# POOL's subtracts and scalings in pieces of 128 or 256 columns, merged V evacuation, and the second key head's rows moved beside the first steps

## The chip, the cores and the metric

The kernel runs on one core of a Trainium2 chip. Its time is the device time of one execution in microseconds (us); for a kernel with several runs it is their median. The engines are named as in the profile: PE (TensorE, matmuls and transposes), PEld (its weight loads), DVE (VectorE), ACT (ScalarE), POOL (GpSimd), SP (SyncE, which issues the DMAs).

## What is computed

A trunk of two layers over 512 latent tokens (a grid of 8 rows by 64 columns) and 256 context tokens, model width 1024. Each layer normalizes and modulates both streams, projects them with one wide matrix, and runs three branches whose gated outputs are merged, projected and added back:

```python
hx = rms_norm(x, norm_w) * (1.0 + scale_x) + shift_x
rq, rk, rv, rg, nq, nk, nv, ng, gq, gk, gv, gg, mg = split_cols(hx @ w_in)
# retention: 4 heads, both directions, chunks of 128, state from the context
# neighbourhood attention: 8 heads of 64, window 8 x 16 with a bias table, plus all context keys
p = softmax(concatenate([q @ k_local * scale + bias, q @ k_ctx * scale]))
# grouped attention: 8 query heads on 2 key heads, rms norm and rotary on q and k
o = softmax(q_g @ k_all.T * scale) @ v_all
m = g_ret * (ret_o @ w_ret_o) + g_na * (na_o @ w_na_o) + g_gqa * (gqa_o @ w_gqa_o)
x = x + gate_x * (m @ w_out)
```

The context stream gets the same treatment in the first layer only; a last rms norm ends the trunk. All is float32.

## The kernel before

**Split operands.** Every matmul operand is split into two parts of the fast 32-bit matmul type, a high part (the rounded value) and a low part (value minus high part). A product of two such operands is three matmuls, high by high, high by low and low by high (L289 to L291); with an attention probability as one operand it is two. ACT makes most high parts, by a copy, and DVE or POOL the low parts, by a subtract.

**Weights.** `_load` (L262 to L277) fetches a 128x1024 block by DMA into `raw` (two buffers) and makes two halves of 512 columns: `whi` by an ACT copy (L273) and `wlo` by a subtract on POOL (L275). In the finishing stages (`lo_dve` set) the second half's subtract goes to DVE. Each part has five buffers, and a load runs one to two blocks ahead of the matmuls. A block's k-th 128 columns are the k-th product's operand (`wk`, L296). In the last stage `load_b` (L1533 to L1540) splits four blocks of the output matrix in the same way.

**Order of work.** PE's order is written by hand: `window()` lays the steps of one attention head (scores, transposes, value products) between projection units, by costs in us. The orders of ACT, DVE and POOL come from a tile scheduler by priority; the weights' splits carry a raised one (`PRI`). The profiled execution goes through: input, statistics and first projections (0 to 60 us), neighbourhood attention of layer 0 (60 to 275), grouped attention (275 to 360), retention, merging and the finish of layer 0 with the layer change around 970, neighbourhood attention of layer 1 (995 to 1170), grouped attention (1170 to 1345), the rest (to 1640) and the finish.

**Neighbourhood attention.** `s_step` (L666 to L691) computes the scores of one of four query blocks of 128 against 512 keys, adds the bias while it takes the row maximum, and after each pair of blocks does negation (L684), exponentials on ACT (L686), reciprocal (L688) and the scaling of the two probability tiles (L691): even block on DVE, odd block on POOL, 512 columns as two groups of 256. `t_step` (L698) transposes them on PE into PSUM, and `split_pt` (L511) makes the high part on ACT (L514) and the low part on DVE (L515), for the value products L714 and L715. L615 and L616 copy rows of K's parts to the other half of the partitions. The context's own scaling (L537, POOL, 256 columns) and its transposes (L545) belong to the steps of layer 0.

**Grouped attention.** `k_fin` (L847 to L854) ends the key path: rotary, then for each of two key heads i the high part (L851, ACT), the low part (L852, DVE) and copies of both to the other 64 partitions (L853, L854, DVE), 64x768 each. `u_v` (L856 to L875) projects V, copies the projection to SBUF (L863), transposes it in blocks of 128 tokens (L868; groups of four and two blocks share a PSUM bank) and evacuates each block by one ACT copy (L872) and one DVE subtract (L873). In `steps` the scores of a query head (L935, L936) leave through DVE (L937, row maximum), two exponentials on ACT (L946), reciprocal (L948) and the scaling of two tiles of 768 columns (L951): the first on DVE, the second on POOL. `t_step` takes 256 keys at a time (L959), `pv_step` multiplies by V (L971). Query heads 0 to 3 (pairs p = 0, 1) read key head 0, the others key head 1. ACT's evacuations behind V's are L1174 in layer 0 and L1206 in layer 1.

## Time and profile before

| | |
|---|---|
| median of 3 runs | 1699.99 us (1697.99 to 1700.96) |
| the profiled execution's own time | 1703.24 us |
| its span, first to last instruction | 1701.5 us |
| mean granted clock of PE | 0.994 |
| busy: PE, DVE, ACT, POOL | 97%, 65%, 47%, 33% |
| read from memory, written | 138.41 MB, 4.19 MB |

PE is the fullest engine. The span is cut into the stages named above; what PE's busy time leaves of a stage is its idle time there. A bracket behind a timeline row tells the idle time ahead of an instruction and what released it.

### The profile page before, as it was taken

The page shows a single profiled execution, that of the slowest core. Times are in us where ns is not written, and L with a number is a line of the kernel's source. Part 1 is how long each engine was busy: PE and PEld are TensorE (multiplying, and loading weights), DVE is VectorE, ACT ScalarE, POOL GpSimd, SP SyncE. Part 2 cuts the span into 40 slices and gives each one's busy share as a digit, 9 for nine tenths or more (in the row PEclk, how much of TensorE's full clock was granted, in tenths as well). Part 3 has the DMA queues.
Part 4 walks back from the last instruction along what each step waited for, and adds up shares of the span by engine and source line. Part 5 has one row for each costly group of instructions (what it writes and reads, how often), then busy time and mean ns, then how long its engine had stood idle before and what let it go on. Part 6 is the DMA issues. An engine that isn't in the chain of part 4 may idle for free. (4 is left out here: it accounts for less than half of the span.)

```text
span 1701.5 us, 24925 instructions
## 1 busy us (share of the span) xinstructions
PE 1642.6 (97%) x9304; PEld 1409.8 (83%) x9304; DVE 1103.7 (65%) x2359; ACT 792.5 (47%) x1561; POOL 556.1 (33%) x482
## 2 busy tenths in 40 slices
PE   6999999999999999999999999999999999999997
PEld 4878888989998888888888889877888888888876
DVE  6666565757654566666768956666776645666775
ACT  4455563645553344443223545653555534444442
POOL 1433322333233222222232433432333333333542
PEclk9999999999999999999999999999999999999999
DMA  8211111111112111112635521211111121221641
GB/s 324 85 50 57 59 38 63 39 38 48 40 38 73 51 50 50 56 57 91 245 118 202 175 90 48 99 50 63 50 50 50 52 85 63 74 74 63 218 154 62
DMA packets 41881, 144.21 MB, mean 85 GB/s; under 512 B 4896, under 2 KB 6048, under 8 KB 40096
## 3 DMA queue, kind: packets, MB, share of 16 engines
q1 hardware_dynamic: 41760, 142.62, 23.6%
q8 instruction: 73, 1.20, 0.3%
q14 instruction: 48, 0.39, 0.1%
HBM read 138.41 MB, written 4.19 MB: 84 GB/s over the span
## 5 line engine op out<-in xcount | busy, mean ns | idle before, releaser
L275 POOL TENSOR_TENSOR wlo<-raw,whi 128x512 fp32r<-128x512 f32 x333 | 445.2, 1341 | 907.8 <-ACT whi L273 861.2
L289 PE MATMUL pj<-hxh,whi 128*128 128x512 f32 (+1 forms) x1232 | 444.9, 361 | 2.0 <-ACT mt L1206 1.9
L291 PE MATMUL pj<-hxh,wlo 128*128 128x512 f32 (+1 forms) x1232 | 429.4, 349 | 0.0
L290 PE MATMUL pj<-hxl,whi 128*128 128x512 f32 (+1 forms) x1232 | 428.2, 348 | 0.0
L273 ACT CAST whi<-raw 128x512 fp32r<-128x512 f32 x352 | 216.2, 619 | 291.2 <-PE pj L290 163.9
L291 PEld LDWEIGHTS pj<-hxh,wlo 128*128 128x128 f32 x1232 | 233.0, 189 | 31.9
L289 PEld LDWEIGHTS pj<-hxh,whi 128*128 128x128 f32 x1232 | 233.4, 189 | 21.2 <-ACT mt L1206 2.3
L290 PEld LDWEIGHTS pj<-hxl,whi 128*128 128x128 f32 x1232 | 233.9, 190 | 19.4
L515 DVE TENSOR_TENSOR pl<-pt,ph 128x512 fp32r<-128x512 f32 (+2 forms) x208 | 126.9, 625 | 54.4 <-ACT ph L514 52.7
L514 ACT CAST ph<-pt 128x512 fp32r<-128x512 f32 (+2 forms) x208 | 107.5, 533 | 65.7 <-PE pt L703 30.1
L289 PE MATMUL pj<-gat,whi 128*128 128x512 f32 (+1 forms) x260 | 91.5, 352 | 1.5 <-ACT mt L1174 1.5
L291 PE MATMUL pj<-gat,wlo 128*128 128x512 f32 (+1 forms) x260 | 89.8, 345 | 0.0
L290 PE MATMUL pj<-gat,whi 128*128 128x512 f32 (+1 forms) x260 | 89.5, 344 | 0.0
L937 DVE TENSOR_SCALAR_CACHE_REDUCE p<-s 128x384 f32<-128x384 f32 x128 | 68.9, 554 | 30.7 <-PE s L936 29.5
L946 ACT ACTIVATE p<-p,nm,rq 128x768 f32<-128x768 f32 x64 | 65.5, 1024 | 47.2 <-DVE nm L944 46.6
L290 PE MATMUL pt<-hxl,whi 128*128 128x512 f32 (+1 forms) x216 | 81.5, 377 | 2.5 <-DVE hxl L480 2.5
L289 PE MATMUL pt<-hxh,whi 128*128 128x512 f32 (+1 forms) x216 | 81.4, 377 | 1.0 <-ACT hxh L479 1.0
L291 PE MATMUL pt<-hxh,wlo 128*128 128x512 f32 (+1 forms) x216 | 80.9, 375 | 0.0
L951 POOL TENSOR_SCALAR p<-p,rc 128x768 f32<-128x768 f32 x32 | 40.3, 1260 | 76.8 <-DVE rc L948 48.4
L515 DVE TENSOR_TENSOR pl<-pf,ph 128x512 fp32r<-128x512 f32 (+1 forms) x56 | 45.4, 811 | 29.8 <-ACT ph L514 29.7
L514 ACT CAST ph<-pf 128x512 fp32r<-128x512 f32 (+1 forms) x56 | 32.9, 588 | 63.2 <-DVE pf L1111 63.2
L959 PE MATMUL pt<-ident,p 128*128 128x128 f32 x384 | 58.5, 273 | 2.0 <-POOL p L951 1.2
(425 smaller groups left out, 3547.4 us busy)
## 6 DMA issues: line engine op xcount, KB each, us to landing
raw<-in_wcol_dram SPq DMA_DIRECT2D x116, 512.0 KB, 3.5
araw<-in_adaw_dram SPq DMA_DIRECT2D x12, 1024.0 KB, 9.7
raw<-in_wbr_dram SPq DMA_DIRECT2D x24, 512.0 KB, 3.5
avw<-in_adav_dram SPq DMA_DIRECT2D x24, 512.0 KB, 3.7
raw<-in_wout_dram SPq DMA_DIRECT2D x24, 512.0 KB, 3.5
raw<-in_wv_dram SPq DMA_DIRECT2D x16, 512.0 KB, 3.5
bias<-in_nabias_dram SPq DMA_DIRECT2D x16, 384.0 KB, 3.0
x<-in_xt_dram SPq DMA_DIRECT2D x8, 384.0 KB, 5.9
```

Source lines behind the costliest of these rows:

```text
L273: nc.scalar.copy(hi, raw[:, c])
L275: lo_eng.tensor_tensor(lo, raw[:, c], f(hi), op=ALU.subtract)
L289: mm(ps, lhsT=sh, rhs=mh, start=start, stop=False)
L290: mm(ps, lhsT=sh, rhs=ml, start=False, stop=False)
L291: mm(ps, lhsT=sl, rhs=mh, start=False, stop=stop)
L514: nc.scalar.copy(ph[:, :n], pt[:, :n])
L515: nc.vector.tensor_tensor(pl[:, :n], pt[:, :n], f(ph[:, :n]), op=ALU.subtract)
L937: nc.vector.tensor_scalar(P[:, jj, kk], s[:, :384], 1.0, -3.0e38, op0=ALU.mult, op1=ALU.max, accum_out=mx[:, i:i + 1])
L946: nc.scalar.activation(P[:, a], P[:, a], AF.Exp, bias=nm[:, a:a + 1], scale=rqe[:, 2 * hf + a:2 * hf + a + 1], accum_out=sm[:, a:a + 1])
L951: eng.tensor_scalar(P[:, a], P[:, a], rc[:, a:a + 1], 1.0, op0=ALU.mult, op1=ALU.mult)
L959: nc.tensor.transpose(pt[:, c:c + 128], st["P"][:, jj, kc:kc + 128], ident)
```

## The change

Five edits. (1) The low half of a weight on POOL (L275) is made by four subtracts of 128 columns, and the same is done in `load_b` (L1540); halves on DVE stay whole. (2) The odd tile's scaling on POOL in the neighbourhood attention (L691) becomes two of 256 columns. (3) The second tile's scaling on POOL in the grouped attention (L951) becomes three of 256 columns. (4) `k_fin` makes the rows of key head 0 only; those of key head 1 are made when the first value product of the first query head is issued. (5) V's evacuation is one ACT copy and one DVE subtract for each group of four or two blocks. No DMA and no matmul is added or removed.

```diff
--- before.py
+++ after.py
@@ -272,7 +272,9 @@
             with tc.high_priority(PRI):
                 nc.scalar.copy(hi, raw[:, c])
                 lo_eng = nc.vector if i == 1 and env.get("lo_dve") else nc.gpsimd
-                lo_eng.tensor_tensor(lo, raw[:, c], f(hi), op=ALU.subtract)
+                for a in range(0, 512, 512 if lo_eng is nc.vector else 128):
+                    b = a + (512 if lo_eng is nc.vector else 128)
+                    lo_eng.tensor_tensor(lo[:, a:b], raw[:, 512 * i + a:512 * i + b], f(hi[:, a:b]), op=ALU.subtract)
             parts.append((hi, lo))
         ready.append((src, parts))
 
@@ -687,8 +689,10 @@
                                              bias=st["nm"][:, i:i + 1], accum_out=st["sm"][:, i:i + 1])
                     nc.vector.reciprocal(st["rc"][:, h], st["sm"][:, h])
                     for i in (j - 1, j):
-                        eng = nc.gpsimd if i % 2 else nc.vector
-                        eng.tensor_scalar(pv_(P, i), pv_(P, i), st["rc"][:, i:i + 1], 1.0, op0=ALU.mult, op1=ALU.mult)
+                        v = pv_(P, i)
+                        for x in (v[:, 0], v[:, 1]) if i % 2 else (v,):
+                            eng = nc.gpsimd if i % 2 else nc.vector
+                            eng.tensor_scalar(x, x, st["rc"][:, i:i + 1], 1.0, op0=ALU.mult, op1=ALU.mult)
 
                 jobs = [(4 + c, 0, [(j, (256, 384, 384, 256)[j] + 128 * c) for j in range(4)]) for c in range(2)]
                 for t in (0, 1, 2, 3):
@@ -845,13 +849,17 @@
             return u_proj(ap_wcol[self.l][CT_GK], G_ALL, self.stats_evac(get, vcol(self.l, V_KN), NT, done, KLAG))
 
         def k_fin(self, kr):
+
             self.rope(kr)
-            for i in range(2):
-                a, b = slice(64 * i, 64 * i + 64), slice(64 - 64 * i, 128 - 64 * i)
-                nc.scalar.copy(self.K1[i][a], kr[a])
-                nc.vector.tensor_tensor(self.K2[i][a], kr[a], f(self.K1[i][a]), op=ALU.subtract)
-                nc.vector.tensor_copy(self.K1[i][b], f(self.K1[i][a]))
-                nc.vector.tensor_copy(self.K2[i][b], f(self.K2[i][a]))
+            self.k_rows(kr, 0)
+            self.late = lambda: self.k_rows(kr, 1)
+
+        def k_rows(self, kr, i):
+            a, b = slice(64 * i, 64 * i + 64), slice(64 - 64 * i, 128 - 64 * i)
+            nc.scalar.copy(self.K1[i][a], kr[a])
+            nc.vector.tensor_tensor(self.K2[i][a], kr[a], f(self.K1[i][a]), op=ALU.subtract)
+            nc.vector.tensor_copy(self.K1[i][b], f(self.K1[i][a]))
+            nc.vector.tensor_copy(self.K2[i][b], f(self.K2[i][a]))
 
         def u_v(self):
             st = {}
@@ -866,11 +874,10 @@
                     pt = bank("s")
                     for i in range(n // 128):
                         nc.tensor.transpose(pt[:, 128 * i:128 * i + 128], vf[:, o + 128 * i:o + 128 * i + 128], ident)
-                    for i in range(n // 128):
-                        v = self.V[:, o // 128 + i]
-                        src = pt[:, 128 * i:128 * i + 128].rearrange("p (h d) -> p h d", h=2)
-                        nc.scalar.copy(v[:, :, 0:64], src)
-                        nc.vector.tensor_tensor(v[:, :, 64:128], src, f(v[:, :, 0:64]), op=ALU.subtract)
+                    v = self.V[:, o // 128:(o + n) // 128]
+                    src = pt[:, :n].rearrange("p (t h d) -> p t h d", h=2, d=64)
+                    nc.scalar.copy(v[:, :, :, 0:64], src)
+                    nc.vector.tensor_tensor(v[:, :, :, 64:128], src, f(v[:, :, :, 0:64]), op=ALU.subtract)
                 defer(VLAG, tr)
             return u_proj(ap_wcol[self.l][CT_GV], G_ALL, ev)
 
@@ -947,8 +954,9 @@
                                                  scale=rqe[:, 2 * hf + a:2 * hf + a + 1], accum_out=sm[:, a:a + 1])
                         nc.vector.reciprocal(rc, sm)
                         for a in range(2):
-                            eng = nc.gpsimd if a else nc.vector
-                            eng.tensor_scalar(P[:, a], P[:, a], rc[:, a:a + 1], 1.0, op0=ALU.mult, op1=ALU.mult)
+                            for c in (slice(0, 256), slice(256, 512), slice(512, 768)) if a else (slice(0, 768),):
+                                eng = nc.gpsimd if a else nc.vector
+                                eng.tensor_scalar(P[:, a, c], P[:, a, c], rc[:, a:a + 1], 1.0, op0=ALU.mult, op1=ALU.mult)
 
                     def t_step(t2, st=st):
                         pt = bank("pt")
@@ -962,6 +970,8 @@
                     def pv_step(t2, e=e, hf=hf, st=st):
                         if t2 == 0:
                             st["ops"] = bank("pv")
+                        if (p, e, hf, t2) == (0, 0, 0, 0):
+                            self.late()
                         ops = st["ops"]
                         ph, pl = st[t2]
                         for x, src in enumerate((ph, pl)):
@@ -1537,7 +1547,10 @@
                 hi, lo = hx[2 * i + j]
                 c = slice(512 * j, 512 * j + 512)
                 nc.scalar.copy(hi[:, :512], raw[:, c])
-                (nc.vector if j else nc.gpsimd).tensor_tensor(lo[:, :512], raw[:, c], f(hi[:, :512]), op=ALU.subtract)
+                for a in range(0, 512, 512 if j else 128):
+                    b = a + (512 if j else 128)
+                    (nc.vector if j else nc.gpsimd).tensor_tensor(lo[:, a:b], raw[:, 512 * j + a:512 * j + b], f(hi[:, a:b]),
+                                                                  op=ALU.subtract)
 
         def gate_rows():
             for h in range(2):
```

## Rows read from the trace of the kernel before

**Rows 1.** View by stretches: PE, PEld, DVE, ACT, POOL busy, PEclk, DMA share, GB/s

```profile
0.00:60.00 60.00, 41.20 (x300) 30.55 (x301) 44.57 (x108) 26.41 (x46) 15.98 (x22) 1.00 0.68 261
60.00:360.00 300.00, 289.60 (x1808) 255.49 (x1806) 192.18 (x452) 155.29 (x352) 94.38 (x101) 0.99 0.15 51
360.00:970.00 610.00, 609.21 (x3588) 535.42 (x3589) 398.87 (x815) 260.21 (x491) 177.46 (x142) 1.00 0.25 90
970.00:995.00 25.00, 21.53 (x128) 19.01 (x127) 20.95 (x43) 10.80 (x22) 10.57 (x13) 0.86 0.27 96
995.00:1190.00 195.00, 185.63 (x1060) 157.74 (x1059) 122.36 (x282) 101.54 (x221) 69.58 (x67) 0.99 0.20 68
1190.00:1640.00 450.00, 444.33 (x2198) 370.37 (x2197) 285.90 (x566) 219.15 (x392) 173.66 (x129) 1.00 0.24 83
1640.00:1701.50 61.50, 51.13 (x232) 41.19 (x231) 38.92 (x96) 19.12 (x40) 14.43 (x11) 0.96 0.23 83
```

**Rows 2.** Waits of PE, whole span: line <- releaser: us, times, longest us

```profile
PE pv L971 <- DVE pl L515: 2.8, 6, 0.8
...
PE s L868 <- ACT sg L863: 2.2, 1, 2.2
PE pj L289 <- ACT mt L1206: 1.9, 1, 1.9
...
PE pj L289 <- ACT mt L1174: 1.5, 1, 1.5
...
PE pt L959 <- POOL p L951: 1.2, 3, 0.4
```

**Rows 3.** Timeline, 102.8 to 106.6 us: start, us, engine line, [idle <-releaser]

```profile
102.85 1.28 POOL L275 TENSOR_TENSOR wlo<-raw,whi 128x512 fp32r<-128x512 f32 x1 [6.07 <-ACT whi L273]
...
103.03 1.38 DVE L616 CAST k<-k 64x512 fp32r<-64x512 f32 x1
...
106.58 0.50 PE L715 MATMUL pv<-pl,v 128*128 128x512 f32 x1 [0.85 <-DVE pl L515]
```

**Rows 4.** Timeline of PE at 235.8 and at 1085.6 us

```profile
235.82 0.78 PE L545 MATMUL pt<-ident,pc 128*128 128x128 f32 x2 [0.79 <-POOL pc L537]
...
1085.59 0.47 PE L674 MATMUL s<-k,q 128*128 128x512 f32 x1 [1.07 <-DVE k L615]
```

**Rows 5.** Timeline of PE at 975.4 us, the change of layers

```profile
975.43 0.50 PE L290 MATMUL pt<-hxl,whi 128*128 128x512 f32 x1 [1.11 <-DVE hxl L480]
```

**Rows 6.** Timeline of POOL and DVE at 18 us, of DVE at 57 us

```profile
17.94 2.51 POOL L275 TENSOR_TENSOR wlo<-raw,whi 128x512 fp32r<-128x512 f32 x2 [1.27 <-ACT whi L273]
18.00 1.24 DVE L205 TENSOR_SCALAR cb<-sel,lg 128x2 f32<-128x2 f32 x1
...
57.17 3.13 DVE L615 CAST k<-k 64x512 fp32r<-64x512 f32 x1
```

**Rows 7.** One line's instructions: count, ns minimum/median/maximum, starts, forms

```profile
L275 POOL TENSOR_TENSOR wlo<-raw,whi x333: 1256/1294/2034, 14.2 to 1656.1; 128x512 fp32r<-128x512 f32 x167
...
L537 POOL TENSOR_SCALAR pc<-pc,rcc x32: 477/478/585, 95.6 to 509.6; 128x256 f32<-128x256 f32 x32
...
L851 ACT CAST gk<-kr x4: 828/834/835, 271.4 to 1177.7; 64x768 fp32r<-64x768 f32 x4
...
L852 DVE TENSOR_TENSOR gk<-kr,gk x4: 944/954/1943, 272.8 to 1180.1; 64x768 fp32r<-64x768 f32 x4
...
L853 DVE CAST gk<-gk x4: 555/556/1515, 273.9 to 1182.1; 64x768 fp32r<-64x768 f32 x4
...
L951 POOL TENSOR_SCALAR p<-p,rc x32: 906/1264/1670, 299.9 to 1352.9; 128x768 f32<-128x768 f32 x32
```

**Rows 8.** Groups by line and form: busy us, mean ns, idle before and releaser

```profile
L515 DVE TENSOR_TENSOR pl<-pt,ph 128x512 fp32r<-128x512 f32 x144 | 97.1, 687 | 48.7 <-ACT ph L514 47.9
...
L515 DVE TENSOR_TENSOR pl<-pf,ph 128x512 fp32r<-128x512 f32 x48 | 42.0, 875 | 26.0 <-ACT ph L514 25.9
...
L872 ACT CAST gv<-s 128x128 fp32r<-128x128 f32 x12 | 3.1, 264 | 9.7 <-DVE gv L873 9.6
```

## The prediction

> **What bounds the kernel.** I read the stretches of the span first. TensorE is busy for nearly all of it: between 360 and 970 us it idles for 0.8 us of 610, so nothing that this change does there can show [rows 1]. Taking PE's busy time from each stretch's length leaves idle time of 18.8 us up to 60, 10.4 from 60 to 360, 3.5 around 980, 9.4 from 995 to 1190, 5.7 from 1190 to 1640 and 10.4 behind that, 59 us in all [rows 1]. The change adds and removes no matmul, so these gaps are all that it can win, with what the clock adds: the stretch around 980 has a granted clock of 0.86, near a stall [rows 1]. The gaps at the start lie under input transfers (DMA share 0.68) and I give them 0.
>
> Next I read whom PE waits for. No row of that view names the weights' low parts on POOL; the waits are for the probabilities' low parts from DVE, for K, for the V path through ACT, and for POOL's scaled probabilities [rows 2]. So POOL's low parts do not hold PE directly. They do it through DVE.
>
> **The hold.** At 102.85 POOL starts a subtract of 1.28 us; 0.18 us later DVE starts a cast of 64x512 that needs 1.38 and ends at 104.41, when POOL has been done for 0.28 us [rows 3]. A larger cast, 64x768, takes 0.556 when nothing holds it, and at most 1.515 [rows 7]. So about 0.9 us of DVE's time went into waiting for POOL, and the low half of the probabilities, queued behind it on DVE, came late: PE stood 0.85 us at 106.58 [rows 3]. Held are DVE's operations with all operands in SBUF. The split of P's transposes shows it: the same 128x512 subtract takes 0.687 us on the mean where it reads PSUM and 0.875 where it reads an SBUF tile [rows 8]. One that reads PSUM is late only because it is queued behind a held one.
>
> **Part 1, pieces of the low parts (L275, L1540).** 333 POOL subtracts of 128x512, 1.256 us at the least, become four of 128x128 each. No row has a POOL subtract of 128 columns. If the time is by column alone a piece takes 0.31 and four take 1.26. If there is a fixed part it follows from the two scalings: 0.477 for 256 columns and 0.906 for 768 at the least, which is 0.84 ns a column and 0.26 us fixed [rows 7]; then 1.256 is 0.26 and 1.95 ns a column, a piece 0.51 and four 2.04. I take the upper side, 0.47 and 1.9, since the fixed part shows in two operations of this engine, though of another kind. POOL's load rises by at most 333 x 0.78 = 260 us, from 556 (the sum of its column [rows 1]) to 816 of 1701: off the path, as no row of PE's waits names its low parts, and PE's k-th product then needs one piece only. No piece waits for more than the whole did (ACT's high part), so nothing new is queued behind a waiting instruction; the pieces of one half stand together in POOL's queue.
>
> What the pieces win is the rest of a hold. A DVE operation that meets a POOL operation at a random point waits on average half of it: 0.65 us of 1.29, 0.24 of a piece, so 6 in 10 of a hold go. I followed each PE wait over 0.2 us back along the chain in order of time, as above, and counted no more of it than the held excess behind it. In the first layer's neighbourhood attention ten waits have 4.5 us of such cause, the first plain one at 106.58, the last at 235.82 [rows 3, 4]; in the second layer four have 1.95, the largest at 1085.59 [rows 4]. 6 in 10 of 6.45 is **-3.9** (0 to -6.5). What is late next there is ACT's high half (L514) or the row maximum, which the change leaves alone; the bound 0 stands for a schedule in which these take over at once. In the grouped attention 2.8 us stand behind DVE's low parts [rows 2], but DVE is fuller there and much of that has no held operation ahead: **-0.9** (0 to -2.8). Around 975 DVE is busy for 20.95 of 25 us [rows 1], and PE waited 1.11 us at 975.43 for its split of the new layer's input, which reads SBUF [rows 5]. 3.5 us of idle time and a slow clock stand there; I take **-2.0** (0 to -5, with the clock). The tail, 10.4 us idle [rows 1], splits the output matrix with half of its low parts on POOL: **-0.4** (-1.2 to +0.5). For the start, 0 (-1.5 to +0.8).
>
> Against this stands POOL's own queue. A scaling of probabilities that is queued directly behind a low part now starts up to 0.6 to 0.8 us later. That happens where PE is near: at 235.82 PE waited 0.79 for such a scaling (L537, not changed itself) [rows 4]. I count two such places in full: **+1.2** (0 to +2.5).
>
> Whether the holds shrink at all depends on who gets in between two pieces. Two POOL subtracts ran back to back from 17.94 for 2.51 us; the DVE operation that met the first was out after 1.24 us, and so it did get in between them [rows 6]. But at 57.17 a cast stood for 3.13 us while POOL ran a row of short operations: there it did not [rows 6]. The Trainium skill (SBUF — State Buffer, section "SBUF: two separate sides") calls the shared port pair an exclusive lock that the earlier of the two instructions keeps to its end. By that every hold would end with one piece (the second rival, below); the case at 18.00 agrees, the 3.13 us at 57.17 do not.
>
> **Part 2, probabilities in pieces (L691, L951).** Two pieces of 256 take 0.96 and three take 1.43, from the 0.477 of a 256-column scaling, against 1.264 at the median for 768 [rows 7]: the last column comes up to 0.2 us later, the first two thirds sooner. PE's first transposes in the grouped attention need the first 256 columns only. PE stood three times, 1.2 us in all, for the whole [rows 2]: **-1.2** (0 to -1.2).
>
> **Part 3, K and V.** Twelve ACT copies of V, 0.264 each, alternate with twelve DVE subtracts on the same PSUM bank; ACT spent 9.6 us waiting between them [rows 8]. Merged, a group is one copy and one subtract, and the ACT operation queued behind (the merge's evacuation, for which PE waited 1.5 us in layer 0 and 1.9 in layer 1 [rows 2]) comes as soon as the copy is done. In layer 0 that wait goes: **-1.5** (0 to -1.5). In layer 1 the subtracts also stood behind the second head's three DVE operations (0.954 and twice a cast of 0.556 [rows 7]), which the change moves away; that wait goes, -2.0, and the copy of the second head's rows, 0.834 on ACT, no longer stands ahead of V's evacuation, for which PE waited 2.2 [rows 2, 7]: -0.85. Together **-2.9** (-1.5 to -4.4, the low end if the clock's dip behind this stall goes too).
>
> The second head's rows come back beside the first value products: ACT 0.83, DVE 0.95 + 0.56 + 0.56 = 2.07 us [rows 7], with no DMA and nothing on SP or POOL. Queued behind them on DVE are the next low halves and row maxima; what hides them is DVE's slack, plentiful at 305, small around 1205, where PE already waits for DVE. If there is no cover the cost is 2.07. I take half: **+1.0** (0 to +2.1). The rows themselves are first read by the second pair of query heads, far later.
>
> **Sum.** -3.9 -0.9 -2.0 -0.4 +1.2 -1.2 -1.5 -2.9 +1.0 = -10.6 us. The profiled execution took 1703.24, so 1692.6; the median of the runs, 1699.99, lies 3.25 below the profiled one, and the same difference gives **1689.4**.
>
> **Rivals.**
> *Only K and V count.* DVE waits through the whole series, as at 57.17 [rows 6], so the pieces are one long operation to it. Then only part 3 is left: -4.4 + 1.0 = -3.4, 1696.6; if the +1.2 of POOL's queue is paid as well, 1697.8. For it speaks the 57.17 row, against it the one at 18.00.
> *Every hold ends with one piece, and the clock with it.* Then all of 6.45 + 2.8 + 1.2 + 3.5 + 4.4 goes, and about 1 us of clock: -19.4, 1680.6. Against it: a wait that goes leaves PE with the next one, and several waits of [rows 2] have no held operation behind them.
> *Slower: alternation.* Pieces and DVE take turns, each piece holding another DVE operation. POOL's time for a low part grows from 1.26 to 2.04, and so does the time in which DVE is held. It decides where DVE has two or more all-SBUF operations queued without a gap, as around 18 [rows 6]. Some 25 PE waits have DVE behind them; at +0.45 each that is +11, less 3.4 of part 3: 1707.6. Against it: in attention most of DVE's queue reads PSUM, and passes.
>
> **How the numbers follow.** Chances: forecast 0.55, only K and V 0.20, every hold 0.12, alternation 0.13. 0.2% is 3.4 us, about what a measurement of this kernel tells from no change; faster then means below 1696.6. The forecast lies almost wholly there, the second half of the first rival's chance beside it: faster 0.74, same 0.15, slower 0.11. The range reaches from the case of all holds, 1681, to past the first rival with its bounds (late rows at +2.1, POOL's queue at +2.5), 1701; the alternation and a little of either end stay out.
>
> **What the profile after would show.** L275 on POOL with some 1332 pieces of 0.31 to 0.51 us. DVE's casts (L615, L616) with maxima under 1 us instead of 1.4: if they stay, the pieces do nothing. The idle time at 970 to 995 under 2 us and the clock near 1 there. No wait for L1174 and L1206 of over 0.5 us, else part 3 is wrong. Three POOL waits of L959 gone. New waits for L537 or around 1205 would be the costs. The forecast is wrong if the holds grow in number as they shrink in size.

## The result and the profile after

The changed kernel takes 1689.45 us at the median (1688.41 to 1690.93, 4 runs) against 1700.47 for the kernel before in the same comparison (1697.99 to 1701.33); the ratio is 0.9935, 95% interval 0.9924 to 0.9947: 11.0 us less. The forecast was 1689.4. Its profiled execution took 1688.41 us with a span of 1686.4, so by the two profiled executions the difference is 14.8 us.

The stretches of the changed kernel first, columns as in [rows 1]. Work comes earlier here by what has been saved, so the stretches do not hold exactly the same work as those of before:

```profile
0.00:60.00 60.00, 41.64 (x310) 31.42 (x311) 44.89 (x112) 26.42 (x46) 21.65 (x49) 1.00 0.68 261
60.00:360.00 300.00, 292.93 (x1834) 259.50 (x1833) 185.24 (x451) 157.87 (x353) 129.46 (x270) 0.99 0.16 53
...
970.00:995.00 25.00, 20.59 (x161) 19.59 (x160) 15.67 (x37) 9.57 (x20) 11.36 (x26) 1.00 0.21 74
995.00:1190.00 195.00, 189.18 (x1066) 159.85 (x1065) 126.87 (x304) 105.69 (x225) 98.01 (x210) 1.00 0.22 72
1190.00:1640.00 450.00, 444.29 (x2199) 370.49 (x2197) 271.98 (x563) 218.00 (x389) 255.47 (x499) 1.00 0.26 86
```

PE's idle time from 60 to 360 fell from 10.4 to 7.1 us, from 995 to 1190 from 9.4 to 5.8, behind 1190 hardly (5.7 either way). The clock is full around 980. DVE is busy for 15.67 us there instead of 20.95, but that is other work: what lay between 970 and 995 us lies between 964.4 and 987.7 in the changed kernel, and there DVE is busy for 19.60 us. POOL's column has grown in every stretch shown.

Whom PE waits for, in the changed kernel (line, releaser, us, times, longest us):

```profile
PE pv L719 <- DVE pl L517: 5.6, 10, 1.0
...
PE pt L967 <- POOL p L959: 2.0, 3, 1.3
PE pt L547 <- POOL pc L539: 1.5, 2, 1.0
PE s L676 <- DVE k L617: 1.4, 4, 0.7
...
PE s L876 <- ACT sg L871: 1.1, 1, 1.1
```

The lines have moved by some places: L967 is the grouped attention's transposes, L871 V's evacuation, L517 the probabilities' low part. Against [rows 2], the waits for the two merge evacuations (1.9 and 1.5 us) are gone and the one for V fell from 2.2 to 1.1. But the one for POOL's scaled probabilities, which part 2 was to remove, rose from 1.2 to 2.0, with one wait of 1.3.

Single lines' instructions in the changed kernel (minimum/median/maximum ns; L617 and L618 are the casts that were L615 and L616, L686 the negation that was L684):

```profile
L277 POOL TENSOR_TENSOR wlo<-raw,whi x1332: 444/463/1447, 14.6 to 1643.6; 128x128 fp32r<-128x128 f32 x191
...
L617 DVE CAST k<-k x16: 289/421/1294, 56.0 to 1111.6; 64x512 fp32r<-64x512 f32 x8, 64x256 fp32r<-64x256 f32 x8
...
L618 DVE CAST k<-k x16: 290/422/1036, 59.1 to 1112.4; 64x512 fp32r<-64x512 f32 x8, 64x256 fp32r<-64x256 f32 x8
...
L686 DVE TENSOR_SCALAR nm<-mx x32: 149/169/621, 76.0 to 1128.8; 128x2 f32<-128x2 f32 x32
```

A piece takes 0.463 us at the median, four of them 1.85, where the forecast took 0.47 and 1.9. The casts' maxima fell, from 3.129 to 1.294 us and from 1.383 to 1.036, but not under the 1 us that the forecast had named. And the place of [rows 3], the cast behind the subtract, in the changed kernel's timeline (start, us, engine, line):

```profile
101.63 1.90 POOL L277 TENSOR_TENSOR wlo<-raw,whi 128x128 fp32r<-128x128 f32 x4 [6.09 <-ACT whi L273]
...
101.81 0.56 DVE L618 CAST k<-k 64x512 fp32r<-64x512 f32 x1
...
103.80 0.68 DVE L517 TENSOR_TENSOR pl<-pt,ph 128x512 fp32r<-128x512 f32 x1
```

The same cast meets the same low part at the same distance (0.18 us behind its start) and takes 0.56 us instead of 1.38: it goes on behind the first piece, although three more follow. PE's wait of 0.85 us that stood behind it is gone. Over the whole run DVE is busy for 1057.9 us instead of 1103.7. About 45 us of this are holds that went (the low parts in pieces alone, below, bring DVE to 1058.9); PE saw a few us of them only.

**Where the time went.** PE runs the same matmuls in the same order in all these kernels (9304 records in each trace), so the n-th of one can be set against the n-th of the other. The table gives, for each kernel of this study, by how much the work of a stretch became shorter (us, negative is shorter) than in the profiled execution of before; the limits are places in the trace of before. It is worked out from the start times of PE's instructions.

```
                    to 60   to 275   to 345   to 500   to 970   to 995  to 1172  to 1192  to 1345  to 1640      end      all
after                -1.2     -2.1     -1.8     -0.3     -0.2     -1.7     -0.3     -4.9     -1.4     -0.6     -0.4    -15.0
changed_again        -1.5     -2.2     -1.8     -0.3      0.5      0.3     -0.3     -4.9     -1.3     -0.6     -0.7    -12.9
kv_only              -0.1      0.2     -1.8     -0.0      0.0      0.4     -0.3     -4.8      0.0     -0.4     -0.9     -7.6
v_merge_only          0.3     -1.3     -1.6     -0.0      0.6      1.0     -0.3     -3.8      0.0     -0.2     -0.7     -6.0
rows_at_once         -1.2     -2.1     -1.8     -0.3     -0.0     -1.5     -0.3     -4.0     -1.5     -0.6     -0.6    -14.0
lo_only              -1.3     -2.4     -0.5     -0.4      0.2      0.5     -0.2     -2.7     -2.0     -0.5     -0.4     -9.6
lo_and_kv            -1.4     -2.3     -1.8     -0.4      0.1     -0.0     -0.7     -5.0     -1.7     -0.6     -0.5    -14.5
lo_and_kv_again      -1.9     -2.5     -1.8     -0.4     -0.3     -1.4     -0.7     -5.0     -1.8     -0.7     -0.4    -17.0
lo_256                0.6     -2.8     -1.8     -0.8     -0.4      0.4     -0.2     -4.9     -2.1     -0.8     -0.7    -13.6
lo_256_kv             0.3     -1.8     -1.8     -0.3     -0.4     -1.0     -1.0     -4.9     -1.9     -0.8     -1.1    -14.8
lo_64                 3.3      3.2     -1.8      1.3      5.4      0.7      3.5     -5.9      1.0      5.0      5.9     21.5
prob_only             0.9     -1.7      0.0     -0.3     -0.0      0.8      0.1      0.0     -0.6     -0.8     -1.0     -2.6
scale_first          -1.1     -3.4     -1.8     -0.9     -0.4     -1.8     -0.6     -5.0     -3.1     -0.7     -0.6    -19.3
```

Three cautions belong to it. Behind 1345 us every kernel but lo_64 gains 0.9 to 1.9, also those that change nothing there (kv_only, v_merge_only): the profiled execution of before was slow by about 1 us in that stretch, as it was above its own median as a whole (1703.24 against 1700.47). From 970 to 995, the change of layers, two executions of one and the same program differ by 1.4 to 2 us (-1.7 and +0.3 for the changed kernel; 0.0 and -1.4 for lo_and_kv). And in the column to 275, v_merge_only gains 1.3 and prob_only 1.7. The clock does most of that: before, it is granted at 0.50 from 88.5 to 91.9 us, behind waits of 0.74 and 0.99, and in the changed kernel too (from 87.3, both executions); in v_merge_only, prob_only and scale_first it stays at 1.00 behind much the same waits. That is worth about 1.3 us and belongs to the execution, not to a change, since v_merge_only changes nothing there. The -3.4 of scale_first has it in it, the -2.1 of the changed kernel has not. Elsewhere between 60 and 1345 two executions of one program agree to 0.3 us, but for 500 to 970, where they differ by up to 0.7.

### The profile page after: what moved, and what is told of

Same layout as the page of the kernel before. It is cut to its first block, busy times and chain, and to the rows that moved or that the text cites. A ratio compares the mean times of both kernels' runs of the same rounds, so it can differ in the third digit from the quotient of the medians.

```text
span 1686.4 us, 26076 instructions
## 1 busy us (share of the span) xinstructions
PE 1634.8 (97%) x9304; PEld 1405.9 (83%) x9304; DVE 1057.9 (63%) x2351; ACT 792.7 (47%) x1553; POOL 806.9 (48%) x1589
## 5 line engine op out<-in xcount | busy, mean ns | idle before, releaser
L277 POOL TENSOR_TENSOR wlo<-raw,whi 128x128 fp32r<-128x128 f32 x1332 | 670.5, 537 | 683.6 <-ACT whi L273 650.0
L292 PEld LDWEIGHTS pj<-hxl,whi 128*128 128x128 f32 x1232 | 233.7, 190 | 19.3
L517 DVE TENSOR_TENSOR pl<-pt,ph 128x512 fp32r<-128x512 f32 (+2 forms) x208 | 126.8, 625 | 59.4 <-ACT ph L516 57.6
L959 POOL TENSOR_SCALAR p<-p,rc 128x256 f32<-128x256 f32 x96 | 55.1, 588 | 62.0 <-DVE rc L955 58.0
L967 PE MATMUL pt<-ident,p 128*128 128x128 f32 x384 | 58.7, 274 | 2.5 <-POOL p L959 2.0
L967 PEld LDWEIGHTS pt<-ident,p 128*128 128x128 f32 x384 | 46.4, 140 | 15.5 <-POOL p L959 3.0
```

Of the source, the lines that this page charges most:

```text
L277: lo_eng.tensor_tensor(lo[:, a:b], raw[:, 512 * i + a:512 * i + b], f(hi[:, a:b]), op=ALU.subtract)
L292: mm(ps, lhsT=sh, rhs=ml, start=False, stop=False)
L517: nc.vector.tensor_tensor(pl[:, :n], pt[:, :n], f(ph[:, :n]), op=ALU.subtract)
L959: eng.tensor_scalar(P[:, a, c], P[:, a, c], rc[:, a:a + 1], 1.0, op0=ALU.mult, op1=ALU.mult)
L967: nc.tensor.transpose(pt[:, c:c + 128], st["P"][:, jj, kc:kc + 128], ident)
```

## Experiments

The theory after the result: three parts, each with its own mechanism. Pieces of the low parts cut DVE's holds; part 3 removes the two stalls around K and V; pieces of the scalings do little. The rivals: that DVE waits through a series of pieces anyway and part 3 alone counts; that pieces and DVE take turns, so that finer is worse. Numbers are medians; ratios are to the kernel before, run on the same chip.

### Part 3 alone (kv_only)

```diff
-            for i in range(2):
-                ...
+            self.k_rows(kr, 0)
+            self.late = lambda: self.k_rows(kr, 1)
...
-                    for i in range(n // 128):
-                        ...
+                    nc.scalar.copy(v[:, :, :, 0:64], src)
+                    nc.vector.tensor_tensor(v[:, :, :, 64:128], src, f(v[:, :, :, 0:64]), op=ALU.subtract)
```

> The kernel before with part 3 alone: merged V evacuation and the second key head's rows beside the first value products; POOL's operations whole. Theory (each part pays for its own waits): the waits for L1174 and L1206 go and the one for V's transposes shrinks by about 0.85; the prediction's sum for it is -4.4 + 1.0 = -3.4 us, 1696.6 to 1697; with the clock's dip behind the layer-1 stall gone as well, -4.4 to -6, 1694.5 to 1696. Rival (only K and V count, the pieces do nothing): the whole difference of the change, -11, 1689.5.

Measured: 1694.19 us against 1700.81, ratio 0.9959 (0.9945 to 0.9973), -6.6. By the table 1.8 us in layer 0 and 4.8 in layer 1, and nothing else between 60 and 970. So the rival falls: part 3 is not the whole -11. But it is worth twice the forecast's -3.4, and a little more than was expected with the clock's dip (1694.5 at the least).

### Low parts in pieces alone (lo_only)

```diff
-                lo_eng.tensor_tensor(lo, raw[:, c], f(hi), op=ALU.subtract)
+                for a in range(0, 512, 512 if lo_eng is nc.vector else 128):
+                    ...
+                    lo_eng.tensor_tensor(lo[:, a:b], raw[:, 512 * i + a:512 * i + b], f(hi[:, a:b]), op=ALU.subtract)
...
```

(The same in `load_b`.)

> The kernel before with the weights' low parts on POOL in four pieces of 128 columns and nothing else. Theory (a held DVE operation waits for one piece): -6 us by the prediction's terms (-3.9, -0.9, -2.0, -0.4, +1.2), 1693 to 1696, and DVE's casts L615/L616 with a maximum under 1 us. Rival (DVE waits through the series): 0, 1699 to 1701, maxima as before (1.4 us). Rival (alternation, each piece holds another operation): 1703 or more.

Measured: 1691.97 us, ratio 0.9945 (0.9933 to 0.9958), -8.8; DVE busy for 1058.9 us. Both rivals fall. The gain is larger than the theory's -6, and the casts' maxima, 1.294 and 1.037 us, stayed above 1. Part of the -8.8 lies where part 3 acts too, since in layer 1 the second head's rows on DVE were themselves held by low parts: L852 took up to 1.943 us, L853 up to 1.515, twice their medians and more [rows 7]. The stretch from 1172 to 1192 gains 2.7 us with pieces alone, 4.8 with part 3 alone and 5.0 with both. So the two do not add there, and -6.6 - 8.8 counts some 2.5 us twice.

### Scalings in pieces alone (prob_only)

```diff
-                        eng.tensor_scalar(pv_(P, i), pv_(P, i), ...)
+                        for x in (v[:, 0], v[:, 1]) if i % 2 else (v,):
+                            eng.tensor_scalar(x, x, ...)
...
-                            eng.tensor_scalar(P[:, a], P[:, a], ...)
+                            for c in (slice(0, 256), slice(256, 512), slice(512, 768)) if a else (slice(0, 768),):
+                                eng.tensor_scalar(P[:, a, c], P[:, a, c], ...)
```

> The kernel before with only the scalings on POOL in pieces of 256 columns. Theory: the three waits of the grouped attention's transposes for POOL go, -1.2 us, 1698 to 1699.5, hard to tell from none; nothing elsewhere. Rival (the fixed part of each piece delays the last one): 0 to +2.

Measured: 1699.68 us, ratio 0.9990 (0.9982 to 0.9999), -1.1, at the edge of what can be told and just above the expected range. One wait of PE for the scaling (0.8 us) is left of the three.

### Second head's rows at once again (rows_at_once)

```diff
-            self.late = lambda: self.k_rows(kr, 1)
+            self.k_rows(kr, 1)
...
-                        if (p, e, hf, t2) == (0, 0, 0, 0):
-                            self.late()
```

> The changed kernel with the second key head's rows made at once again, behind the first head's; V stays merged, POOL stays in pieces. Theory (these rows stand on ACT ahead of V's evacuation and on DVE ahead of V's subtracts in layer 1): +1 to +2.5 us against the changed kernel, 1690.5 to 1692, and the wait for V's transposes is back near 2.2 us. Rival (merging V alone had freed the merge's evacuation, and the rows cost as much in the new place): 1689 to 1690.

Measured: 1691.53 us, ratio 0.9943 (0.9930 to 0.9955), about 2 us above the changed kernel (1689.45 and, in a second comparison, 1688.85); the intervals overlap, and the trace is clearer. From 1172 to 1192 it gains 4.0 instead of 4.9, and the wait for V is 2.0 us again. So the theory's range held. The price in the new place, the forecast's +1.0, is to be read behind that: from 1192 to 1345 the two differ by 0.1.

### Merged V alone (v_merge_only)

```diff
-                    for i in range(n // 128):
-                        ...
+                    nc.scalar.copy(v[:, :, :, 0:64], src)
+                    nc.vector.tensor_tensor(v[:, :, :, 64:128], src, f(v[:, :, :, 0:64]), op=ALU.subtract)
```

> The kernel before with the merged V evacuation alone; the second key head's rows stay behind the first's. Theory: the wait for L1174 in layer 0 goes (-1.65); in layer 1 V's one subtract still stands behind the second head's rows on DVE, but the copy on ACT does not wait for it, so the wait for L1206 (-2.0) goes too and the wait for V's transposes (2.2) stays: -3.5 to -4, 1696.5 to 1697.3; moving the rows is then worth the rest of part 3's -6.6, about 2.5 with the clock. Rival (the rows are what counts): -1.7, 1699.

Measured: 1698.43 us, ratio 0.9988 (0.9979 to 0.9997), -2.3; the expectation was missed by over a us. Its trace has 1.6 us gained in layer 0 and 3.8 in layer 1, as expected, but 1.6 lost from 500 to 995, where it changes nothing: there the clock is granted at 0.50 for 10.2 us from 975.1, against 6.8 before from 979.4. The waits for L1174 and L1206 are gone and the one for V is 2.2 us as before. So the merging carries the greater share of part 3 by the trace; by the medians the shares stay uncertain.

### Pieces of 256 and of 64 (lo_256, lo_64)

```diff
-                for a in range(0, 512, 512 if lo_eng is nc.vector else 128):
-                    b = a + (512 if lo_eng is nc.vector else 128)
+                for a in range(0, 512, 512 if lo_eng is nc.vector else 256):
+                    b = a + (512 if lo_eng is nc.vector else 256)
```

(64 in the place of 256 for the other; L1552 in the same way.)

> The changed kernel with POOL's low parts in two pieces of 256 columns. Theory (a held DVE operation waits for the rest of one piece): a piece takes about 0.75 us instead of 0.46, the mean wait for its rest is 0.37 instead of 0.23 (0.64 for a whole one), so about a third of the low parts' gain is lost: +2 to +3 us against the changed kernel, 1691.5 to 1692.5. Rival (turns: each piece holds an operation, fewer pieces are better): 1687 to 1689, below the changed kernel.

> The changed kernel with POOL's low parts in eight pieces of 64 columns. From 1.256 us for 512 columns and 0.444 for 128 a piece of 64 takes about 0.31 and eight take 2.5. Theory (rest of one piece): the mean wait falls from 0.23 to 0.15, -0.5 to -1 us, but POOL's scalings queued behind a low part start 0.6 us later, and low parts run late where loads follow each other every 3.4 us: in all 0 to +4, 1689.5 to 1693.5. Rival (turns): +10, 1700.

Measured: 1687.41 us, ratio 0.9924 (0.9910 to 0.9937), with pieces of 256; and 1723.71, ratio 1.0140 (1.0126 to 1.0154), with pieces of 64: 23 us slower than before. Neither of the theory's ranges held. The first number lies in the range of its rival (turns), the second far beyond either; the traces speak against turns all the same, since DVE's busy time falls with the size of the pieces, 1103.0 (kv_only), 1065.8, 1057.9 and 1054.1 us for 512, 256, 128 and 64 columns: smaller pieces do not hold DVE for longer in all. But two pieces relieve it of 37 us where four relieve it of 45, more than the two thirds that the theory of the rest of a piece had. The prices are as worked out, one line's instructions of the two kernels, pieces of 256 first:

```profile
L277 POOL TENSOR_TENSOR wlo<-raw,whi x666: 714/739/1784, 14.8 to 1643.8; 128x256 fp32r<-128x256 f32 x167
```

```profile
L277 POOL TENSOR_TENSOR wlo<-raw,whi x2664: 307/322/1300, 14.7 to 1680.6; 128x64 fp32r<-128x64 f32 x191
...
L686 DVE TENSOR_SCALAR nm<-mx x32: 149/170/2370, 80.6 to 1152.0; 128x2 f32<-128x2 f32 x32
```

What is new is the last number: an operation of 0.17 us took up to 2.37, longer than with whole low parts (1.187, the maximum that the same line, L684, has in the kernel before). The timeline of the kernel with pieces of 64 at that place:

```profile
80.06 4.23 POOL L277 TENSOR_TENSOR wlo<-raw,whi 128x64 fp32r<-128x64 f32 x15
...
80.63 2.37 DVE L686 TENSOR_SCALAR nm<-mx 128x2 f32<-128x2 f32 x1
...
83.66 0.50 PE L676 MATMUL s<-k,q 128*128 128x512 f32 x1 [1.75 <-DVE mx L679]
```

Fifteen pieces follow one another every 0.28 us. The operation does not get in between them; it comes out after eight of them, and PE waits 1.75 us for what is queued behind it. Near the end a subtract of 0.69 us is held for longer still, through eleven pieces, though PE is not waiting at that place (the same kernel):

```profile
1635.94 5.80 POOL L277 TENSOR_TENSOR wlo<-raw,whi 128x64 fp32r<-128x64 f32 x17
...
1637.08 3.75 DVE L1532 TENSOR_TENSOR mhl<-m,mhl 128x512 fp32r<-128x512 f32 x1 [4.07 <-ACT mhl L1531]
```

So the case of [rows 6] at 57.17, a cast of 3.13 us, was no oddity. Nor was it a matter of short operations alone, as the prediction has it; POOL's row at that place in the kernel before holds a whole low part:

```profile
57.04 0.73 POOL L586 MEMSET kz<- 64x768 f32 x1
57.74 1.28 POOL L275 TENSOR_TENSOR wlo<-raw,whi 128x512 fp32r<-128x512 f32 x1
58.96 0.30 POOL L657 MEMSET bias<- 128x256 f32 x1
...
59.72 0.30 POOL L660 MEMSET pb<- 128x256 f32 x1
```

So DVE can be passed over at the seam of two POOL operations. Pieces of 0.463 us let the cast at 101.81 in, and most operations must get in between pieces of 0.32 too, else DVE's busy time would not be at its lowest there; a few sit through a series. What decides which of them do stays open.

By PE's waits, most of the 23 us lies elsewhere. Eight pieces of 64 take about 2.25 us against 1.29 for a whole low part, POOL is busy for 1059 us, and where the loads follow one another closely it does not keep up: from 1584.96 it runs 56 pieces in 23.82 us without a pause. Then everything that needs POOL comes late. PE's waits in this kernel:

```profile
PE pj L291 <- DVE mt L1237: 6.1, 1, 6.1
...
PE pt L967 <- POOL p L959: 5.4, 5, 2.2
PE pt L547 <- POOL pc L539: 4.0, 3, 1.5
...
PE pt L422 <- DMA araw<-in_adaw_dram: 3.4, 1, 3.4
PE s L1525 <- DMA xo<-x_mid: 3.3, 1, 3.3
...
PE pt L324 <- POOL wlo L277: 2.4, 2, 1.9
```

The changed kernel has 1.1, 2.0 and 1.5 us in the first three and none of the last three. The 6.1 stands behind a late transfer: ACT waited 4.17 us for a weight's before it could go on. SP, which issues the transfers in order and needs POOL's last piece before it may fill a weight's buffer again, waits 495.6 us for POOL instead of 336.4; that the late transfers come from there is likely, not shown. The clock adds three stretches of 3.4 us at 0.50, at 60.2, 845.3 and 1087.6, and one of 6.8 at 1664.5, that neither execution of the changed kernel has. How the 23 us divide between held DVE operations, POOL's own queue and the clock was not measured apart.

### Low parts in pieces and part 3, scalings whole (lo_and_kv, twice), and the changed kernel beside it

```diff
-                        for x in (v[:, 0], v[:, 1]) if i % 2 else (v,):
-                            ...
+                        eng.tensor_scalar(pv_(P, i), pv_(P, i), ...)
...
-                            for c in (slice(0, 256), slice(256, 512), slice(512, 768)) if a else (slice(0, 768),):
-                                ...
+                            eng.tensor_scalar(P[:, a], P[:, a], ...)
```

> The changed kernel with the scalings of probabilities on POOL whole again: low parts in pieces plus part 3. Alone, part 3 gave -6.6 us and the low parts -8.8. Theory (both act on one stall, that of layer 1's K and V, where the low parts alone recover 2.7 us and part 3 4.8 of some 5): they don't add; -11 to -13 together, 1688 to 1690, and the stretch around the K and V of layer 1 gains 5, not 7.5. Rival (they are independent and the scalings' pieces cost the difference): -15.4, 1685.5.

Measured: 1685.5 us against 1700.76, ratio 0.9920 (0.9908 to 0.9933), -15.3. By the median the rival (independent parts, the scalings' pieces costing the difference) was right; by the trace the theory, which has the stretch from 1172 to 1192 at -5.0 and not at -7.5. So both were run again, on one chip:

> The changed kernel itself, beside the next two on one chip, so that they are compared with it and not across chips. Theory: 1688.5 to 1690.5, -11 us. What it tells: whether the 4 us by which the kernel with whole scalings was faster belong to the scalings' pieces (then -11 again here, and -15 there), or to the spread between chips and runs (then the two within 1.5 us of each other).

> Low parts in four pieces and part 3, scalings of probabilities whole. Theory A (pieces of the scalings cost in company of the low parts' pieces, since three of them hold DVE again and stand behind a longer series): 1684.5 to 1686.5, 3 to 4 us under the changed kernel. Theory B (no effect, as the traces have the two within 0.6 us of each other up to 1345 us): within 1.5 us of it.

Measured: 1688.85 us for the changed kernel (0.9928, 0.9916 to 0.9941), 1686.74 for the one with whole scalings (0.9924, 0.9912 to 0.9936). The medians are 2 us apart, between the two expectations, and the intervals overlap almost fully. That the scalings' pieces won nothing beside the other parts is safe; that they cost is likely. With pieces of 256 and whole scalings (the edits of lo_256 and of lo_and_kv together) it is the same level:

> Low parts on POOL in two pieces of 256 columns, part 3, scalings whole. With four pieces and pieces of the scalings 1689.5, with two 1687.4, with four and whole scalings 1685.5. If both differences are real and add, 1683.5; if two pieces lose a third of the low parts' gain as first expected, 1688; if all of these are one level, 1686 to 1689.

Measured: 1686.35 us, 0.9919 (0.9905 to 0.9932). Of the expectations, the last held: four pieces or two can't be told apart, and no sum of small differences is to be had here.

### Scalings' pieces kept together (scale_first)

Why did part 2 give nothing? The changed kernel's timeline of POOL around 1230 us, and what PE waited for:

```profile
1229.04 1.70 POOL L277 TENSOR_TENSOR wlo<-raw,whi 128x128 fp32r<-128x128 f32 x4
1230.72 2.60 POOL L959 TENSOR_SCALAR p<-p,rc 128x256 f32<-128x256 f32 x5
...
1231.25 0.55 PE L967 MATMUL pt<-ident,p 128*128 128x128 f32 x3 [1.26 <-POOL p L959]
```

The row ahead of these is a single piece of L959, started at 1228.17. The five that follow the low part are the other two of this scaling and the three of the next. So one piece of a scaling was ordered ahead of the low part and two behind it: the low parts' priority is higher, and the scheduler could put them between two pieces of a scaling, which it could not while the scaling was one operation. It needs no pieces of the low parts for that: in prob_only a whole low part of 1.27 us stands at the same place behind the first piece (1241.14), and PE waits 0.83 us there. The last experiment gives the pieces of the grouped attention's scalings the higher priority and changes nothing else:

```diff
-                                eng.tensor_scalar(P[:, a, c], P[:, a, c], ...)
+                                with tc.high_priority(HP if a else 0):
+                                    eng.tensor_scalar(P[:, a, c], P[:, a, c], ...)
```

> The changed kernel with the three pieces of the grouped attention's scaling given a higher priority than the weights' low parts, so that no low part is ordered in between the pieces of one scaling. Theory (with pieces the scheduler puts four subtracts of a low part between the first and the second piece, as at 409 to 415 and 1228 to 1233 us of the changed kernel, and PE waits 0.28 and 1.26 us there): these two waits go; the grouped attention gains 0.6 us near 415 and 0.95 near 1230 against the changed kernel and keeps the 0.3 to 0.9 won near 355 and 1285; in all -1.5, about 1687.5 against 1689. Rival (the pieces cost by holding DVE more often, not by their order): the steps at 415 and 1230 stay, within 0.5 us of the changed kernel.

Measured: 1686.58 us against 1700.58, ratio 0.9917 (0.9903 to 0.9930). POOL around the same place, in this kernel's timeline:

```profile
1225.69 1.80 POOL L960 TENSOR_SCALAR p<-p,rc 128x256 f32<-128x256 f32 x3 [3.76 <-DVE rc L955]
1227.47 1.71 POOL L277 TENSOR_TENSOR wlo<-raw,whi 128x128 fp32r<-128x128 f32 x4
1229.17 0.78 POOL L960 TENSOR_SCALAR p<-p,rc 128x256 f32<-128x256 f32 x1
```

and of PE's waits for POOL:

```profile
PE pt L968 <- POOL p L960: 0.4, 1, 0.4
```

The three pieces stand together, and of 2.0 us of waiting 0.4 are left. Set instruction against instruction with the changed kernel, it gains 0.5 us near 412 and 1.5 near 1230, and next to nothing elsewhere in the grouped attention: from 345 to 500 and from 1192 to 1345 it has -0.9 and -3.1 where the changed kernel has -0.3 and -1.4. The theory holds, by the trace. (Another 1.3 of its -19.3 is the clock at 88 us, see the cautions at the table, and no merit of the change.) This is also the kernel with the lowest ratio of the study; its interval touches that of the changed kernel (0.9924 to 0.9947 in the one comparison, 0.9916 to 0.9941 in the other), so it is faster than the kernel before for certain, and faster than the changed one by the trace and by 2.3 to 2.9 us of medians, not beyond the spread of the runs.

## Why the prediction was right, step by step

**The time** came out as forecast, 1689.45 against 1689.4. That it agrees to a tenth is luck: by the profiled executions the sum was short by 2 to 4 us, and the constant that carried it over to the median was wrong by as much the other way (see the total). The mechanisms of the holds and of K and V were right, though not every size; those of the scalings and of POOL's queue were not.

**Holds in the neighbourhood attention**, -3.9, and POOL's queue, +1.2, so -2.7 in all: measured -2.1 in layer 0 and -0.3 in layer 1 (two executions agree), -2.4. As a sum it is right, and the cast of [rows 3] shows the mechanism of the first term. Matmul by matmul, five places in layer 0 (at 106.6, 139.1, 152.2, 211.8 and 229.5 of before) give -2.4 and three in layer 1 (1085.6, 1119.9, 1166.4) -1.0, half of the 6.45 where 6 in 10 were taken. They do not each shrink by half: the waits at 106.6 and 139.1 are gone, while those at 148.8 and 208.4, 1.05 and 1.04 us, stayed as they were. The queue's term did not come where it was put. With the low parts alone in pieces (lo_only) the wait at 235.82 is 0.79 us as before, and PE's waits for the context's scalings fall to 0.8 in total. They are back at 1.5, with 1.02 at that place, only with the probabilities' scalings in pieces too (prob_only: 1.7). What is left of the sum, about +1.0, so comes mostly from part 2.

**The price of a piece**: 0.463 and 1.85 against 0.47 and 1.9. The four sizes, 1.256, 0.714, 0.444 and 0.307 us at the least for 512, 256, 128 and 64 columns, give 2.1 ns a column and 0.17 us fixed; POOL's load became 807 us, forecast at most 816.

**K and V**: layer 0 -1.8 against -1.5. In layer 1, -4.9 against -2.9, beyond the lower bound of -4.4. The term that was too small is the clock's. Before, it fell behind this stall, and the changed kernel at the same work has it full (the stretch view, 1187.6 to 1191 us of the kernel before, and 1175 to 1179 of the changed one):

```profile
1187.60:1191.00 3.40, 3.40 (x10) 2.83 (x9) 0.03 (x1) 0.62 (x1) 0.89 (x2) 0.50 0.44 153
```

```profile
1175.00:1179.00 4.00, 4.00 (x20) 3.44 (x19) 1.75 (x6) 0.62 (x1) 3.90 (x9) 1.00 0.42 131
```

Granted 0.50 is the lower of the two levels, 1.2 GHz. Matmul by matmul the waits for V and the merge give -1.15 and -2.2 and the clock -1.6. So the two steps of the sum were short by 0.5 together, and the return of the clock, kept for the bounds, belonged into the sum: the fall followed the stall in the trace of before, and does so again in prob_only (1187.2), which leaves the stall as it is; no other kernel has it.

**The late rows**, +1.0: about 0.1, by rows_at_once. The forecast took the middle between no cover and full cover. With whole low parts (kv_only) the same stretch, 1192 to 1345, shows no cost either (0.0), so DVE's slack was there before the holds were cut.

**The scalings**, -1.2: the step that failed. The wait for the whole scaling was real, and all but gone (0.4 us) where pieces stay together (scale_first). But "POOL's queue" was thought of as a queue in which the scaling keeps its place; that its pieces could be split up by a higher priority was not considered. PE's waits there were 1.2 us before, 0.8 with the scalings alone in pieces, 1.6 with the low parts alone and 2.0 with both. So POOL's longer low parts cost 0.4 here: this, and not the place that the prediction named, is what its term for POOL's queue came to.

**The grouped attention's holds**, -0.9: with the scalings, -0.3 in layer 0 and -1.4 in layer 1 against a sum of -2.1. Low parts alone give -0.4 and -2.0, so the holds' term was too small here (2.4) and the scalings' took 0.7 back.

**The change of layers**, -2.0: can't be told. -1.7 in one execution and +0.3 in the other of the same program. The signs were missed: PE idles for 4.4 us from 970 to 995 (3.5 before), not under 2, and the same work keeps DVE busy for 19.60 us, hardly less than the 20.95 of before. The clock makes much of the difference: granted at 0.50 for 6.8 us before (from 979.4) and in the changed kernel's second execution (from 974.8), at 1.00 throughout in its first. But in the first PE then waited 2.5 us for a normalization's factor, held behind other POOL operations, and gave back what had been won:

```profile
975.39 1.52 POOL L588 MEMSET kz<- 64x768 f32 x2
...
976.74 1.44 DVE L218 SCALAR_TENSOR_TENSOR rs_t<-rs_t,rs_x 128x2 f32<-128x2 f32 x1
...
976.88 1.69 POOL L277 TENSOR_TENSOR wlo<-raw,whi 128x128 fp32r<-128x128 f32 x4
...
979.95 0.71 PE L465 MATMUL s<-ident,rstd 128*128 128x128 f32 x4 [2.52 <-DVE rstd L219]
```

In lo_only, where nothing was won here, a weight's transfer was late as well: its high half waited 2.86 us for it, the changed kernel's 0.37. Here a short operation stood behind the rest of a memset and three pieces: the passing-over happens with four pieces of 0.45 us as well, but this is one of few cases.

**The tail**, -0.4: measured -0.4, but this can't be told: kv_only and v_merge_only, which change nothing there, have -0.9 and -0.7.

**The start**, 0: -1.2 and -1.5, within its bounds. The gap does not lie under transfers alone. Two operations of DVE on the way to the second modulation, of 1.46 and 1.24 us in the kernel before, at 44.23 and 45.61, take 0.63 and 0.42 in the changed kernel. Pieces of 256 do not win it.

**The total.** By the profiled executions the change gave -14.8, and -12.7 with the second one (1690.52), against a sum of -10.6; by the medians -11.0. About 1 of the difference is the slow tail of the profiled execution of before; then come the clock (-1.6) and the start (-1.3), which the sum had at 0, and the late rows, which cost 0.1 and not 1.0; against them stands the scalings' failed -1.2. What carried the sum over to the median was no constant: the profiled execution of before lay 3.25 us above the median that the prediction had, those of the changed kernel 1.0 below and 1.7 above theirs. With the first of them the sum was short by 4.2 us and the constant off by 4.3, with the second by 2.1 and 1.6; that the two cancel is luck.

**The rivals.** "Only K and V" is refuted at 128 columns by lo_only (-8.8), "every hold and the clock" by the waits that are left (PE still waits 5.6 us for the probabilities' low parts in the neighbourhood attention). "Slower" named turns of pieces and DVE; that did not occur at 128, and at 64 what occurs is another thing, POOL's fuller queue and a few series that DVE sits through, at about three times the price that the rival had named: +23 us against the kernel before, not +8.

## What to carry to other kernels

A long operation of an engine that is itself off the path can cost by what it holds up on another; cutting it pays as long as the waiting engine gets in between the pieces and the cut engine still keeps up with its own work, and both are to be tested with one finer cut, since the next halving here turned 11 us won into 23 us lost. An operation that is cut becomes several for the scheduler as well: look whether something of higher priority is put between its pieces, and keep the pieces together. When two changes act on one stall, their gains taken alone do not add.

## What the runs showed of the hardware

A DVE operation with all operands in SBUF that waits for POOL does not always get its turn at the end of one POOL operation. Between two subtracts ([rows 6], at 18) and between pieces of 0.463 us (101.81) it did; between a memset and a subtract of 1.28 (57.17) and in one case among pieces of 0.45 (976.74) it did not, and in series of pieces of 0.32 us single operations took up to 3.83, one of 3.75 through eleven of them. The rule of the Trainium skill (SBUF — State Buffer, section "SBUF: two separate sides") that the lock is kept to the end of one instruction describes the former; it does not foresee the latter.
